# Turning and scaling a normalised tile in one matrix product, in a two-layer-pair transformer kernel

## The chip, the cores and the metric

The kernel runs on one core of a Trainium2 chip. The metric is device time in microseconds (us) of one execution. The kernel before takes 2766.55 us, the median of three runs (2766.45 to 2769.73). Its profile comes from one further execution, which took 2766.35 us.

## The reference, cut to what matters

The reference is two transformer blocks over 256 tokens of width 1024, each with two layers. Every layer has a mixer and a second part (cross attention and a lookup of experts in the first block, a gated feed-forward in the second). In front of each of these parts stands a root-mean-square norm:

```python
def rmsnorm(x, g):
    xf = x.astype(jnp.float32)
    y = xf * lax.rsqrt(jnp.mean(xf * xf, axis=-1, keepdims=True) + EPS)
    return (y * g.astype(jnp.float32)).astype(x.dtype)

hn = rmsnorm(h, mix_norm[l])
h = h + short_conv_pool_mixer(hn, ...)      # starts with hn @ w_in
h = h + memory_cross_attn(rmsnorm(h, xattn_norm[l]), ...)
h = h + peer_ffn(rmsnorm(h, peer_norm[l]), ...)
```

Ten such norms are each followed at once by a product of the normed rows with a weight matrix. The result is float32, and the products are made from float32 data.

## The kernel before, in words

The residual `h` lies in SBUF as two row blocks of 128 tokens by 1024. Each float32 operand of a large product is split into a high part (`hi`, `xh`: the value rounded to the matmul's fp32r format) and a low part (`lo`, `xl`: what is left). One product of float32 numbers is then three fp32r products: high by high, high by low, low by high (`mm3`).

A norm (`norm_T`, `norm_steps`) turns `h` from rows of tokens to columns of tokens. For each row block b, every row is scaled by its factor `r` (the reciprocal root, made by a DVE addition in `rstd`, L220, and a power on GpSimd, L221). The scaled block `xn` (128x1024) is then transposed by TensorE in eight pieces of 128x128 (L266), piece k of both blocks going into columns 0 to 255 of one PSUM bank. There are eight banks: mm0, mm1, tp0, tp1, a0 to a3, one for each piece k. After both blocks, `hilo_ps` empties each bank k twice: ScalarE (ACT) writes the high part `xh` with the gain of the norm (L283), then VectorE (DVE) writes the low part `xl` (L284).

Block 0 of `xn` is scaled by DVE alone (L250, 1024 wide). For block 1 the left half is scaled by DVE (L253) and the right half by ACT (L254). The norm of the first mixer has both factors ready when it begins (`done == 2`). The other nine have only that of block 0 (`finish`, which adds the last products to `h`, makes it), and the factor of block 1 is made inside the norm. In the norm in front of the second block's first mixer a closure in `self.second` makes it, with a second power.

Weights come by DMA on SyncE's queue into a ring `raw` of four buffers, and `_split` makes `hi` (ACT, L114) and `lo` (DVE, L117) from them, in rings of three. `w(name, j)` keeps the splits three blocks ahead of use. In the nine norms, one `_split` stands between the factor of block 1 and its scaling: ACT's L114, then both scalings, then DVE's L117.

After a norm comes, in most stages, `columns`: a result of 128 weight columns by 256 tokens in one PSUM bank, accumulated over eight pieces k, with three products for each k (L152, L153, L154 in `mm3`). Its first call follows the norm directly, so its products wait for `xh` and `xl` of each k. The mixer in front of which the closure stands begins instead with products in the other orientation (weights as the moving operand), through `mm3`.

The order on each engine is the order in which the program is written (a manual schedule); a layer under it adds the semaphore waits that data and buffers ask for. No planner chooses the order.

Of the kernel before, what the change touches and what calls it, by code (L numbers as in the profile page):

```python
# [20 lines left out]
F32 = mybir.dt.float32  # L21
# [4 lines left out]
AF = mybir.ActivationFunctionType  # L26
OP = mybir.AluOpType
# [47 lines left out]
class Program:  # L75
# [23 lines left out]
        self.raw[i] = t  # L99
        self.n_dma += 1  # L100

    def _split(self, between=None):
        if self.order is None or self.n_split == len(self.order):
            if between:
                between()
            return
        i = self.n_split
        w = self.order[i][2]
        while self.n_dma <= i:
            self._load()  # L110
        raw = self.raw.pop(i)
        hi = self.ring.tile([128, w], F32R, name="hi", bufs=self.HL)
        lo = self.ring.tile([128, w], F32R, name="lo", bufs=self.HL)
        self.nc.scalar.activation(hi, raw, AF.Copy)  # L114
        if between:
            between()
        self.nc.vector.tensor_tensor(lo, raw, hi.bitcast(F32), OP.subtract)  # L117
        self.split[i] = (hi, lo)
        self.n_split += 1

# [35 lines left out]
    def columns(self, ps, name, j, xT, k_n=8):  # L156

        hi, lo = self.w(name, j, 128 * k_n)
        for k in range(k_n):
            s = slice(k * 128, (k + 1) * 128)  # L160
            self.mm3(ps, hi[:, s], lo[:, s], xT[0][:, k, :], xT[1][:, k, :], k == 0, k == k_n - 1)

    def rows(self, name, ks, xT, acc, gain=None, fine=False):

# [64 lines left out]
    def norm_T(self, src, gain, xn=None, fill=0):  # L229

        hi, lo = [self.act.tile([128, 8, 256], F32R, name=f"x{i}", bufs=1) for i in "hl"]
        done, self.normed = self.normed, 1
        if xn is not None:
            for _ in self.norm_steps(src, gain, hi, lo, self.ss, xn, self.r, done):
                self.fill(fill)
            return hi, lo
        self.n_norm += 1
        with self.tc.tile_pool(name=f"norm{self.n_norm}", bufs=1) as tmp:
            xn = tmp.tile([128, 2, 1024], F32, name="xn")
            for _ in self.norm_steps(src, gain, hi, lo, self.ss, xn, self.r, done):  # L240
                self.fill(fill)
        return hi, lo

    def norm_steps(self, src, gain, hi, lo, ss, xn, r, done=1):

        nc = self.nc
        pss = [(self.ps_mm() if k < 2 else self.ps_tp() if k < 4 else self.ps_a(k - 4))[:, :256] for k in range(8)]
        for b in range(2):
            if b == 0:
                nc.vector.tensor_scalar(xn[:, b], src[:, b], r[:, 1, b:b + 1], None, op0=OP.mult)  # L250
            else:
                def scale():
                    nc.vector.tensor_scalar(xn[:, b, :512], src[:, b, :512], r[:, 1, b:b + 1], None, op0=OP.mult)  # L253
                    nc.scalar.activation(xn[:, b, 512:], src[:, b, 512:], AF.Copy, scale=r[:, 1, b:b + 1])  # L254

                if done < 2:
                    second, self.second = self.second, None
                    if second:
                        second()
                    else:  # L260
                        self.rstd(r, ss, 1)
                    self._split(scale)
                else:
                    scale()
            for k in range(8):
                nc.tensor.transpose(pss[k][:, b * 128:(b + 1) * 128], xn[:, b, k * 128:(k + 1) * 128], self.ident)  # L266
        first = done == 2 and not self.asked
        for k in range(8):
            if first and k in (0, 4):
                self._split()  # L270
            self.hilo_ps(hi[:, k, :], lo[:, k, :], pss[k], gain[:, k:k + 1])
        yield

    def hilo(self, hi, lo, src):
        self.nc.scalar.activation(hi, src, AF.Copy)  # L275
# [463 lines left out]
    def odd_mixer(self, pool):  # L739
# [44 lines left out]
        for j in range(8):  # L784
            if j == 1:
                ps = turned(ckvT)
                for b in range(2):
                    x = ps[:, b * 128:(b + 1) * 128]
                    nc.scalar.activation(ckv[:, b], x, AF.Copy)
                    self.square_sum(self.const.tile([128, 512], BF, name="scr", bufs=2)[:, :128], ckv[:, b], st[:, b:b + 1], 0)  # L790
                self.power(st[:, 2:4], st[:, 0:2], 128)
            next(columns)
            if j == 2:
                for b in range(2):
                    v.scalar_tensor_tensor(ckv[:, b], ckv[:, b], st[:, 2 + b:3 + b], self.kv_norm, op0=OP.mult, op1=OP.mult)
            if j:
                for _ in range(2):
                    next(select, None)
            yield
# [874 lines left out]
```

## Time and profile before

| what | value |
|---|---|
| median of 3 runs | 2766.55 us (2766.45 to 2769.73) |
| the profiled execution | 2766.35 us, span 2764.3 us |
| PE busy | 2691.8 us, 97% |
| DVE busy | 1993.0 us, 72% |
| ACT busy | 1344.7 us, 49% |
| POOL busy | 66.0 us, 2% |
| mean DMA rate | 168 GB/s |

The span runs from the first to the last instruction of the program; the execution's own time is 2.05 us longer. Busy time of an engine is a sum over its instructions; PE is the matmuls of TensorE, PEld its weight loads, POOL is GpSimd, SP is SyncE. In rows of a timeline, "idle before" and an arrow name what the engine waited for.

### The profile page before, as it was taken

The page shows a single profiled execution, that of the slowest core. Times are in us where ns is not written, and L with a number is a line of the kernel's source. Part 1 is how long each engine was busy: PE and PEld are TensorE (multiplying, and loading weights), DVE is VectorE, ACT ScalarE, POOL GpSimd, SP SyncE. Part 2 cuts the span into 40 slices and gives each one's busy share as a digit, 9 for nine tenths or more (in the row PEclk, how much of TensorE's full clock was granted, in tenths as well). Part 3 has the DMA queues.
Part 4 walks back from the last instruction along what each step waited for, and adds up shares of the span by engine and source line. Part 5 has one row for each costly group of instructions (what it writes and reads, how often), then busy time and mean ns, then how long its engine had stood idle before and what let it go on. Part 6 is the DMA issues. An engine that isn't in the chain of part 4 may idle for free.

```text
span 2764.3 us, 50311 instructions
## 1 busy us (share of the span) xinstructions
PE 2691.8 (97%) x20160; PEld 2453.7 (89%) x20160; DVE 1993.0 (72%) x3741; ACT 1344.7 (49%) x2275; POOL 66.0 (2%) x109
## 2 busy tenths in 40 slices
PE   8999999999999999999999999999999889998998
PEld 7889999998888878978999999888887879987997
DVE  7457788898996556855778889899656765557654
ACT  5455445434444555555544543444455554446543
POOL 2000000000000001010000000000000100000000
PEclk9999999999999999999999999999999999999999
DMA  6645555544555556443555554555555525543454
GB/s 225 214 127 170 184 183 178 165 154 162 165 167 187 191 184 197 137 130 124 174 183 183 178 164 152 165 163 166 188 192 177 180 77 179 187 161 100 160 183 145
DMA packets 127338, 463.32 MB, mean 168 GB/s; under 512 B 14912, under 2 KB 15192, under 8 KB 126336
## 3 DMA queue, kind: packets, MB, share of 16 engines
q1 hardware_dynamic: 122688, 445.31, 49.3%
q0 software_dynamic: 3776, 14.40, 1.7%
q8 instruction: 158, 2.59, 0.4%
q14 instruction: 76, 0.62, 0.1%
q10 hardware_dynamic: 640, 0.40, 0.0%
HBM read 456.64 MB, written 3.34 MB: 166 GB/s over the span
## 4 chain that ended last, share of the span: by engine, by line
PE 90%; DVE 4%; ACT 3%; issue 1%; DMA 1%; POOL 0%; POOLq 0%; ACTq 0%; SPq 0%; DVEq 0%
PE mm L152 16%; PE mm L153 16%; PE mm L154 16%; PE a L152 12%; PE a L154 11%; PE a L153 11%; PE tp L704 3%; DVE lo L117 1%; ACT hi L114 1%; PE a L458 1%; DVE ap L485 1%; PE tp L554 1%; ACT ap L487 1%; PE a L996 0%; PE a L446 0%
## 5 line engine op out<-in xcount | busy, mean ns | idle before, releaser
L117 DVE TENSOR_TENSOR lo<-raw,hi 128x1024 fp32r<-128x1024 f32 (+2 forms) x847 | 1033.4, 1221 | 604.0 <-ACT hi L114 600.9
L114 ACT ACTIVATE hi<-raw 128x1024 fp32r<-128x1024 f32 (+2 forms) x847 | 889.6, 1050 | 522.3 <-PE a L154 495.9
L152 PE MATMUL mm<-xh,hi 128*128 128x256 f32 x3584 | 1026.8, 286 | 3.3 <-DVE xl L284 2.6
L153 PE MATMUL mm<-xl,hi 128*128 128x256 f32 x3584 | 1015.3, 283 | 0.5 <-DVE xl L284 0.5
L154 PE MATMUL mm<-xh,lo 128*128 128x256 f32 x3584 | 1014.3, 283 | 0.9 <-DVE lo L117 0.9
L152 PEld LDWEIGHTS mm<-xh,hi 128*128 128x128 f32 x3584 | 688.0, 192 | 7.1 <-DVE xl L284 4.9
L153 PEld LDWEIGHTS mm<-xl,hi 128*128 128x128 f32 x3584 | 688.1, 192 | 0.9 <-DVE xl L284 0.7
L154 PEld LDWEIGHTS mm<-xh,lo 128*128 128x128 f32 x3584 | 687.7, 192 | 1.3 <-DVE lo L117 1.3
L152 PE MATMUL a<-hi,xh 128*128 128x512 f32 x1072 | 424.7, 396 | 1.6 <-ACT xh L275 1.6
L154 PE MATMUL a<-hi,xl 128*128 128x512 f32 x1072 | 418.2, 390 | 0.0
L153 PE MATMUL a<-lo,xh 128*128 128x512 f32 x1072 | 417.0, 389 | 0.0
L580 ACT ACTIVATE A<-mm 128x256 f32<-128x256 f32 x256 | 104.7, 409 | 437.2 <-PE mm L154 437.2
L154 PEld LDWEIGHTS a<-hi,xl 128*128 128x128 f32 x1072 | 201.2, 188 | 43.6 <-DVE xl L276 0.3
L152 PEld LDWEIGHTS a<-hi,xh 128*128 128x128 f32 x1072 | 201.4, 188 | 41.7 <-ACT xh L275 2.0
L153 PEld LDWEIGHTS a<-lo,xh 128*128 128x128 f32 x1072 | 201.6, 188 | 40.1
L696 DVE TENSOR_TENSOR go<-o,gT 128x512 bf16<-128x512 bf16 x384 | 140.3, 421 | 4.4
L704 PEld LDWEIGHTS <-o 128*128 128x128 bf16 x3072 | 96.7, 98 | 19.5 <-issue 16.7
L704 PE MATMUL tp<-go,o 128*128 128x64 bf16 x3072 | 111.8, 193 | 0.0
L276 DVE TENSOR_TENSOR xl<-A,xh 128x256 fp32r<-128x256 f32 x256 | 106.4, 417 | 2.0 <-ACT xh L275 2.0
L275 ACT ACTIVATE xh<-A 128x256 fp32r<-128x256 f32 x256 | 105.9, 415 | 0.0
L691 DVE TENSOR_TENSOR o<-iota,slot 128x1024 bf16<-128x1024 bf16 x128 | 87.6, 685 | 0.0
L709 DVE TENSOR_TENSOR A<-tp,A 128x512 f32<-128x512 f32 x128 | 87.6, 685 | 0.0
(473 smaller groups left out, 2530.8 us busy)
## 6 DMA issues: line engine op xcount, KB each, us to landing
raw<-pu SPq DMA_DIRECT2D x256, 512.0 KB, 3.7
raw<-pv SPq DMA_DIRECT2D x256, 512.0 KB, 4.3
raw<-fgu SPq DMA_DIRECT2D x88, 512.0 KB, 3.3
raw<-fdown SPq DMA_DIRECT2D x44, 512.0 KB, 3.3
raw<-pwq SPq DMA_DIRECT2D x32, 512.0 KB, 3.7
raw<-ein SPq DMA_DIRECT2D x16, 512.0 KB, 5.4
raw<-eout SPq DMA_DIRECT2D x16, 512.0 KB, 3.5
raw<-xwk SPq DMA_DIRECT2D x16, 512.0 KB, 4.4
```

Source lines behind the costliest of these rows:

```text
L114: self.nc.scalar.activation(hi, raw, AF.Copy)
L117: self.nc.vector.tensor_tensor(lo, raw, hi.bitcast(F32), OP.subtract)
L152: mm(out, ah, bh, start=start, stop=False)
L153: mm(out, ah, bl, start=False, stop=False)
L154: mm(out, al, bh, start=False, stop=stop)
L275: self.nc.scalar.activation(hi, src, AF.Copy)
L276: self.nc.vector.tensor_tensor(lo, src, hi.bitcast(F32), OP.subtract)
L580: self.nc.scalar.activation(A[:, c // 2, :, c % 2], ps, AF.Gelu_apprx_tanh)
L691: v.tensor_tensor(o2, iota[:, None].to_broadcast([128, 8, 64, 2]), slot[:, 1, t, None].to_broadcast([128, 8, 64, 2]), OP.is_equal)
L696: v.tensor_tensor(go[:, k], o1, gT[:, k, t, None].to_broadcast([128, 8, 32, 2]), OP.mult)
L704: nc.tensor.matmul(ps[:, j, :], o2[:, j].rearrange("p n two -> p (n two)"), go[:, k, j].rearrange("p n two -> p (n two)"), start=k == 0, s ...
L709: v.tensor_tensor(a, prod.pop(i).rearrange("p t (c two) -> p t c two", two=2), a, OP.mult)
```

## The change

Instead of scaling a row block and transposing it, the norm multiplies each 128x128 piece of `h`, as it is, with a diagonal matrix of the 128 factors. The product turns and scales the piece in one. DVE makes the diagonal (128x128) from the identity matrix and `r`. The eight pieces now lie in four PSUM banks (tp0, tp1, a0, a1), two to a bank: pieces 0 and 1 in the first, 2 and 3 in the second. The low part of the one weight block that is split inside the norm is made by GpSimd instead of DVE, and ACT no longer scales anything. In `columns`, the product with the low part of x comes one piece later than before, and the product with the low part of the weight takes its place.

```diff
@@ -99,10 +99,8 @@
         self.raw[i] = t
         self.n_dma += 1
 
-    def _split(self, between=None):
+    def _split(self, engine=None):
         if self.order is None or self.n_split == len(self.order):
-            if between:
-                between()
             return
         i = self.n_split
         w = self.order[i][2]
@@ -112,9 +110,7 @@
         hi = self.ring.tile([128, w], F32R, name="hi", bufs=self.HL)
         lo = self.ring.tile([128, w], F32R, name="lo", bufs=self.HL)
         self.nc.scalar.activation(hi, raw, AF.Copy)
-        if between:
-            between()
-        self.nc.vector.tensor_tensor(lo, raw, hi.bitcast(F32), OP.subtract)
+        (engine or self.nc.vector).tensor_tensor(lo, raw, hi.bitcast(F32), OP.subtract)
         self.split[i] = (hi, lo)
         self.n_split += 1
 
@@ -156,9 +152,14 @@
     def columns(self, ps, name, j, xT, k_n=8):
 
         hi, lo = self.w(name, j, 128 * k_n)
+        mm = self.nc.tensor.matmul
         for k in range(k_n):
             s = slice(k * 128, (k + 1) * 128)
-            self.mm3(ps, hi[:, s], lo[:, s], xT[0][:, k, :], xT[1][:, k, :], k == 0, k == k_n - 1)
+            mm(ps, hi[:, s], xT[0][:, k, :], start=k == 0, stop=False)
+            mm(ps, lo[:, s], xT[0][:, k, :], start=False, stop=False)
+            if k:
+                mm(ps, hi[:, (k - 1) * 128:k * 128], xT[1][:, k - 1, :], start=False, stop=False)
+        mm(ps, hi[:, s], xT[1][:, k, :], start=False, stop=True)
 
     def rows(self, name, ks, xT, acc, gain=None, fine=False):
 
@@ -231,45 +232,38 @@
         hi, lo = [self.act.tile([128, 8, 256], F32R, name=f"x{i}", bufs=1) for i in "hl"]
         done, self.normed = self.normed, 1
         if xn is not None:
-            for _ in self.norm_steps(src, gain, hi, lo, self.ss, xn, self.r, done):
-                self.fill(fill)
+            self.norm_steps(src, gain, hi, lo, xn[:, 0, :256].rearrange("p (b t) -> p b t", b=2), self.r, done)
+            self.fill(fill)
             return hi, lo
         self.n_norm += 1
         with self.tc.tile_pool(name=f"norm{self.n_norm}", bufs=1) as tmp:
-            xn = tmp.tile([128, 2, 1024], F32, name="xn")
-            for _ in self.norm_steps(src, gain, hi, lo, self.ss, xn, self.r, done):
-                self.fill(fill)
+            self.norm_steps(src, gain, hi, lo, tmp.tile([128, 2, 128], F32, name="diag"), self.r, done)
+            self.fill(fill)
         return hi, lo
 
-    def norm_steps(self, src, gain, hi, lo, ss, xn, r, done=1):
+    def norm_steps(self, src, gain, hi, lo, diag, r, done):
+
 
         nc = self.nc
-        pss = [(self.ps_mm() if k < 2 else self.ps_tp() if k < 4 else self.ps_a(k - 4))[:, :256] for k in range(8)]
+        banks = [self.ps_tp() if k < 2 else self.ps_a(k - 2) for k in range(4)]
+        pss = [banks[k // 2][:, k % 2 * 256:k % 2 * 256 + 256] for k in range(8)]
         for b in range(2):
-            if b == 0:
-                nc.vector.tensor_scalar(xn[:, b], src[:, b], r[:, 1, b:b + 1], None, op0=OP.mult)
-            else:
-                def scale():
-                    nc.vector.tensor_scalar(xn[:, b, :512], src[:, b, :512], r[:, 1, b:b + 1], None, op0=OP.mult)
-                    nc.scalar.activation(xn[:, b, 512:], src[:, b, 512:], AF.Copy, scale=r[:, 1, b:b + 1])
-
-                if done < 2:
-                    second, self.second = self.second, None
-                    if second:
-                        second()
-                    else:
-                        self.rstd(r, ss, 1)
-                    self._split(scale)
+            if b >= done:
+                second, self.second = self.second, None
+                if second:
+                    second()
                 else:
-                    scale()
+                    self.rstd(r, self.ss, 1)
+                self._split(self.nc.gpsimd)
+            nc.vector.tensor_scalar(diag[:, b], self.ident, r[:, 1, b:b + 1], None, op0=OP.mult)
             for k in range(8):
-                nc.tensor.transpose(pss[k][:, b * 128:(b + 1) * 128], xn[:, b, k * 128:(k + 1) * 128], self.ident)
+                nc.tensor.matmul(pss[k][:, b * 128:(b + 1) * 128], src[:, b, k * 128:(k + 1) * 128], diag[:, b],
+                                 start=True, stop=True)
         first = done == 2 and not self.asked
         for k in range(8):
             if first and k in (0, 4):
                 self._split()
             self.hilo_ps(hi[:, k, :], lo[:, k, :], pss[k], gain[:, k:k + 1])
-        yield
 
     def hilo(self, hi, lo, src):
         self.nc.scalar.activation(hi, src, AF.Copy)
```

On ACT, in the norm in front of the last feed-forward part, one `xh` for each piece. Before (`xn` is the scaled block, the first names of the reads are PSUM banks):

```order
L114 ACTIVATE hi_29069<-raw_28832 128x1024 [waits DMAHW3_49,PE_49]
L254 ACTIVATE xn_29049<-h_71,rstd_29001 128x512 [waits Pool_49]
L283 ACTIVATE xh_29044<-mm1_29050,g_g_ffn_182 128x256 [waits PE_49]
L283 ACTIVATE xh_29044<-mm0_29051,g_g_ffn_182 128x256 [waits PE_49]
L283 ACTIVATE xh_29044<-tp0_29052,g_g_ffn_182 128x256 [waits PE_49]
L283 ACTIVATE xh_29044<-tp1_29053,g_g_ffn_182 128x256 [waits PE_49]
```

The same place on ACT now:

```order
L112 ACTIVATE hi_29020<-raw_28787 128x1024 [waits DMAHW3_49,PE_49]
L277 ACTIVATE xh_28999<-tp0_29005,g_g_ffn_177 128x256 [waits PE_49]
L277 ACTIVATE xh_28999<-tp0_29005,g_g_ffn_177 128x256 [waits DVE_49]
L277 ACTIVATE xh_28999<-tp1_29006,g_g_ffn_177 128x256 [waits PE_49]
L277 ACTIVATE xh_28999<-tp1_29006,g_g_ffn_177 128x256 [waits DVE_49]
L277 ACTIVATE xh_28999<-a0_29007,g_g_ffn_177 128x256 [waits PE_49]
```

The scaling L254 is gone, each bank is now read twice, and the second read of each bank has a wait on DVE where it had one on PE.

On GpSimd, the factors of the last three norms and of the output norm (each `x2` is one power for each row block). Before:

```order
L221 TENSOR_TENSOR rstd_25948<-rstd_25948,mhalf_88 128x1 [waits DVE_49] x2
L221 TENSOR_TENSOR rstd_27895<-rstd_27895,mhalf_88 128x1 [waits DVE_49,Pool_49]
L221 TENSOR_TENSOR rstd_27895<-rstd_27895,mhalf_88 128x1 [waits DVE_49]
L221 TENSOR_TENSOR rstd_29001<-rstd_29001,mhalf_88 128x1 [waits DVE_49] x2
L221 TENSOR_TENSOR rstd_30932<-rstd_30932,mhalf_88 128x1 [waits DVE_49] x2
```

The same place on GpSimd now:

```order
L222 TENSOR_TENSOR rstd_25913<-rstd_25913,mhalf_88 128x1 [waits DVE_49] x2
L113 TENSOR_TENSOR lo_25978<-raw_25750,hi_25977 128x1024 [waits DMAHW7_49,Activation_49,Pool_49]
L222 TENSOR_TENSOR rstd_27855<-rstd_27855,mhalf_88 128x1 [waits DVE_49] x2
L113 TENSOR_TENSOR lo_27921<-raw_27797,hi_27920 128x1024 [waits DMAHW1_49,Activation_49,Pool_49]
L222 TENSOR_TENSOR rstd_28956<-rstd_28956,mhalf_88 128x1 [waits DVE_49] x2
L113 TENSOR_TENSOR lo_29021<-raw_28787,hi_29020 128x1024 [waits DMAHW3_49,Activation_49,Pool_49]
```

The weight's low part now stands on GpSimd right behind the power that makes the factor of block 1, and it waits for ACT's high part.

On PE, the first products of `columns` behind the same norm. Before:

```order
L152 MATMUL mm1_29102<-xh_29044,hi_28993 128x256 [waits DVE_49]
L153 MATMUL mm1_29102<-xl_29045,hi_28993 128x256
L154 MATMUL mm1_29102<-xh_29044,lo_28994 128x256
L152 MATMUL mm1_29102<-xh_29044,hi_28993 128x256 [waits Activation_49]
L153 MATMUL mm1_29102<-xl_29045,hi_28993 128x256 [waits DVE_49]
L154 MATMUL mm1_29102<-xh_29044,lo_28994 128x256
```

The same place on PE now:

```order
L158 MATMUL mm1_29052<-xh_28999,hi_28948 128x256 [waits Activation_49]
L159 MATMUL mm1_29052<-xh_28999,lo_28949 128x256
L158 MATMUL mm1_29052<-xh_28999,hi_28948 128x256 [waits Activation_49]
L159 MATMUL mm1_29052<-xh_28999,lo_28949 128x256
L161 MATMUL mm1_29052<-xl_29000,hi_28948 128x256 [waits DVE_49]
```

The first product now waits for ACT alone, and the product with `xl` of a piece stands behind two products of the next piece.

## Rows read from the trace of the kernel before

**Rows 1.** The page: the span, and the chain of work that ended last, by engine.
```profile
span 2764.3 us, 50311 instructions
...
PE 90%; DVE 4%; ACT 3%; issue 1%; DMA 1%; POOL 0%; POOLq 0%; ACTq 0%; SPq 0%; DVEq 0%
```

**Rows 2.** Timeline, last feed-forward norm: start us, duration us, engine, line, operation, operands.
```profile
2565.03 1.04 ACT L114 ACTIVATE hi<-raw 128x1024 fp32r<-128x1024 f32 x1
...
2565.45 0.55 POOL L221 TENSOR_TENSOR rstd<-rstd,mhalf 128x1 f32<-128x1 f32 x1 [2.04 <-DVE rstd L220]
...
2566.04 0.49 DVE L253 TENSOR_SCALAR xn<-h,rstd 128x512 f32<-128x512 f32 x1 [0.66 <-POOL rstd L221]
2566.44 1.22 DVE L117 TENSOR_TENSOR lo<-raw,hi 128x1024 fp32r<-128x1024 f32 x1
...
2566.58 0.44 PE L266 MATMUL mm<-ident,xn 128*128 128x128 f32 x2 [0.40 <-DVE xn L253]
...
2566.95 0.84 ACT L283 ACTIVATE xh<-mm,g_g_ffn 128x256 fp32r<-128x256 f32 x2 [0.19 <-PE mm L266]
...
2567.57 0.87 DVE L284 SCALAR_TENSOR_TENSOR xl<-mm,g_g_ffn,xh 128x256 fp32r<-128x256 f32 x2
...
2569.14 1.65 DVE L284 SCALAR_TENSOR_TENSOR xl<-a,g_g_ffn,xh 128x256 fp32r<-128x256 f32 x4
...
2571.19 0.29 PE L152 MATMUL mm<-xh,hi 128*128 128x256 f32 x1
```

**Rows 3.** Stages: bounds, length, busy (count) of PE, PEld, DVE, ACT, POOL, PEclk, DMA, GB/s.
```profile
8.68:16.30 7.62, 7.00 (x40) 6.40 (x39) 6.38 (x13) 6.59 (x12) 7.25 (x11) 1.00 0.83 275
138.48:143.77 5.29, 4.91 (x38) 4.28 (x37) 4.85 (x10) 4.04 (x10) 0.00 (x0) 1.00 0.54 185
205.91:211.10 5.19, 4.38 (x35) 3.94 (x33) 4.99 (x11) 4.74 (x11) 0.15 (x1) 1.00 0.75 289
...
1244.53:1250.48 5.95, 5.50 (x35) 5.38 (x33) 5.63 (x11) 4.74 (x11) 0.00 (x0) 0.71 0.28 88
...
2144.56:2147.00 2.44, 1.76 (x10) 1.67 (x9) 2.23 (x5) 1.88 (x5) 2.21 (x5) 0.50 0.06 14
...
2469.41:2475.54 6.13, 5.79 (x36) 5.15 (x35) 6.04 (x12) 4.74 (x11) 0.00 (x1) 0.72 0.28 86
2566.00:2571.19 5.19, 4.36 (x34) 3.94 (x33) 4.99 (x11) 4.98 (x12) 0.00 (x1) 1.00 0.34 104
```

**Rows 4.** Timeline of DVE, window attention: scaling of a 128x128 tile.
```profile
2484.51 0.29 DVE L498 TENSOR_SCALAR ap<-ap,ast 128x128 f32<-128x128 f32 x1
```

**Rows 5.** Timeline of PE, cross attention: plain float32 products of 128 columns.
```profile
170.46 1.28 PE L458 MATMUL a<-apT,V 128*128 128x128 f32 x10
```

**Rows 6.** Timeline, window attention: two halves of one PSUM bank, copied by ACT and DVE.
```profile
2478.90 0.22 ACT L300 ACTIVATE vS<-tp 128x64 f32<-128x64 f32 x1
2479.15 0.22 DVE L301 COPY vS<-tp 128x64 f32<-128x64 f32 x1 [0.82 <-ACT vS L300]
2479.41 0.22 ACT L300 ACTIVATE vS<-tp 128x64 f32<-128x64 f32 x1 [0.29 <-DVE vS L301]
```

**Rows 7.** One line's instructions (L929, GpSimd sums): ns min/median/max, forms.
```profile
L929 POOL TENSOR_TENSOR ba<-bias,add x16: 454/739/1723, 1083.5 to 1194.8; 128x128 f32<-128x128 f32 x8, 128x256 f32<-128x256 f32 x8
```

**Rows 8.** Timelines at three places: a GpSimd operation beside a DVE scaling.
```profile
7.52 0.74 DVE L250 TENSOR_SCALAR xn<-h,rstd 128x1024 f32<-128x1024 f32 x1
7.68 0.99 POOL L221 TENSOR_TENSOR rstd<-rstd,mhalf 128x1 f32<-128x1 f32 x1 [0.90 <-DVE rstd L220]
...
1151.88 0.74 POOL L929 TENSOR_TENSOR ba<-bias,add 128x256 f32<-128x256 f32 x1 [4.75 <-DVE ast L497]
1151.91 0.80 DVE L498 TENSOR_SCALAR ap<-ap,ast 128x128 f32<-128x128 f32 x1
...
1184.05 0.64 DVE L498 TENSOR_SCALAR ap<-ap,ast 128x256 f32<-128x256 f32 x1
1184.09 0.45 POOL L929 TENSOR_TENSOR ba<-bias,add 128x128 f32<-128x128 f32 x1 [1.43 <-DVE ast L497]
```

## The prediction

> **What bounds the kernel now.** I read the page first, then the timeline of one norm, then the stages between a norm's last factor and the second column of products behind it, and at the end single lines for the prices. The chain that ended last is PE for 90% [rows 1]: a product saved or delayed on PE is saved or delayed in the end. PE waits in few places, and the ten norms are among them, because everything behind a norm needs its result. The reader should see in [rows 2] the chain of a plain norm. GpSimd's power ends at 2566.00 (2565.45 and 0.55). DVE scales at 2566.04, the first transpose of block 1 starts at 2566.58, ACT's first `xh` at 2566.95, DVE's first `xl` at 2567.57, and the second column of products starts at 2571.19. That is 5.19 us from the power, the length of that stage in [rows 3]. There are five such plain stages of 5.18 to 5.19 us, of which the first and the last are shown. In between, PE follows the evictions: DVE's last four `xl` end at 2570.79 (2569.14 and 1.65), 0.40 before the second column.
>
> The other five are the very first norm (8.68), the first cross attention (138.48), two in which the granted clock fell, with a mean of 0.71 and 0.72 (1244.53 and 2469.41), and the one whose factor takes a second power (2144.56, at 0.50, the lower of the two levels, 1.2 GHz) [rows 3].
>
> **The change part by part.** *The scaling.* L253, L254 and L250 go; two diagonals of 128x128 come. A DVE scaling of that shape took 0.29 us [rows 4] against 0.49 for L253 [rows 2]. The diagonal of block 1 starts 0.04 behind the power as L253 did, so it ends at 2566.33, and the first product starts 0.05 later, at 2566.38: 0.20 us won. The diagonal of block 0 lies beside the sums of block 1 and decides nothing.
>
> *The products.* Sixteen plain float32 products replace sixteen transposes. Ten of them with 128 columns took 1.28 us [rows 5]; with 0.27 for the last one alone that is a step of 0.11, so eight take about 0.9 us and cost what transposes cost. The Trainium skill, page "TensorE: Matmul & The Clock Gate", section Terms, speaks against this: it calls the transpose mode four times faster for FP32. By that rule a product would take some 0.43 us as an estimate (four steps of 0.11), and the second product of each bank would come about 0.3 us later in each norm, some 3 us in all ten. The row disagrees, and the sum goes by the row.
>
> *The banks.* This is the term that decides. Two pieces now share a bank, and in the order on ACT the second `xh` of each bank waits for DVE. In the trace two halves of one bank were copied in the same manner: ACT at 2478.90, DVE at 2479.15, ACT again at 2479.41, each 0.03 or 0.04 after the end of the other (0.22 each) [rows 6]. So the reads of a bank go in turns, ACT, DVE, ACT, DVE, while before, with a bank for each piece, ACT ran ahead. One `xl` takes 0.48 and each further one 0.39 (two in 0.87, four in 1.65); an `xh` by the same division of 0.84 takes 0.46 [rows 2]. A pair is then `xl` 0.48, a gap of 0.03, `xh` 0.46, a gap of 0.03, and 0.40 until the next bank's first `xl` can follow: 1.40 us for two pieces, against 0.78 before.
>
> The plain norm comes out so. First product 2566.38; the bank must be written fully, so 0.11 for the second product and 0.37 from a product's start to `xh` (2566.58 to 2566.95): `xh` at 2566.86. First `xl` at 2567.35 (0.46 and 0.03). Three pairs of 1.40 bring 2571.55. The last pair, up to the end of its second `xl` (0.48, 0.03, 0.46, 0.03, 0.48), brings 2573.03. The second column follows 0.28 later, not 0.40, since one product instead of two stands behind the last `xl`: 2573.31, or 7.31 us from the power. Against 5.19 that is 2.12 us lost.
>
> *The low part one piece later.* It lets the first products start on `xh` alone, and saves the 0.12 just counted. In all later columns nothing waits, the products are as many, and each loads its weights as before (34 products, 33 loads [rows 3]); cost nothing. If the new order slowed each product, no cover would exist, as PE is the bound.
>
> *The weight's low part on GpSimd.* DVE loses L117 (1.22 us, 2566.44 to 2567.66), which held back the first `xl`; that gain is in the 2567.35. On GpSimd 128 columns took 0.454 and 256 took 0.74 [rows 7, 8], 2.23 ns a column, so 1024 take about 2.45 us. It starts when ACT's L114 is done (2566.07) and ends near 2568.6; the second column, which reads it first, starts at 2573.31. So it is hidden unless it disturbs DVE. Behind it on GpSimd wait only loads and later factors. Bounds for a disturbed `xl`: no row shows a DVE operation that reads PSUM beside a long GpSimd one; at least nothing, at most a wait to 2568.6 for the first `xl`, 1.25 us in each norm. I take nothing, because the bank's gaps already stand in that time.
>
> *The exceptional norms.* The first cross attention: 7.31 less 5.29 is 2.0. The very first norm has the same pairs: 2.1. In the two with a fallen clock, six products at 1.2 GHz take 1.28 us (six times 256 columns), less than a pair; so 7.31 less 5.95 and less 6.13, 1.4 and 1.2. In the one with two powers, ACT's high part is long ready, so GpSimd begins the low part (832 columns, 2.0 us by the same slope) straight behind the power, ahead of DVE, which still has one small operation to do before the diagonal. [Rows 8] shows what then happens: L498 started 0.03 behind GpSimd's L929 and took 0.80 instead of 0.29, ending 0.09 after it. The diagonal comes about 1.6 late; its products in the other orientation use pieces more slowly than the pairs deliver; 0.4 come back from the missing L254. I take 1.2, between nothing and 2.0.
>
> Sum: five times 2.12 is 10.6; with 2.0, 2.1, 1.4, 1.2 and 1.2 it is 18.5. The profiled execution took 2766.35, 0.2 below the median of 2766.55: 2784.85, so 2785.
>
> **The rivals.** *A: GpSimd takes DVE's port in the other norms too.* In the plain norm L114 ends at 2566.07, 0.03 after the diagonal starts at 2566.04 [rows 2]: a race. A lead of 0.16 for DVE was enough once (7.52 against 7.68: the power had to wait and took 0.99 instead of 0.55), a lead of 0.04 was not (1184.05 against 1184.09: the scaling took 0.64, the GpSimd sum ran undisturbed) [rows 8]. The lead here is 0.03 plus whatever GpSimd needs to start behind ACT, so between the two. If it is lost, the diagonal ends 0.09 after GpSimd, at 2566.07 and 2.45 and 0.09, 2568.61 instead of 2566.33: 2.3 us in each norm. Three lost give 2792, seven 2801. The Trainium skill says the same on the page "SBUF — State Buffer", section "SBUF: two separate sides": whichever of the two starts first holds the shared port pair for its whole instruction. The rows agree.
>
> *B: the clock.* With the pairs, PE stands half idle for over five us in each norm, more than before, and a norm with a fallen clock was 0.76 and 0.94 longer than a plain one [rows 3]. If seven more norms leave the pairs at the lower level and pay 0.9 after it, that is 6.3 us: 2791. Against it: five of ten held the clock through a longer full stop.
>
> *C: not slower.* The wait on DVE in the order finds its operation done, or the bank does not take turns. Then the `xl` run on at 0.39: from 2567.35 seven steps and 0.48 bring 2570.56 and the second column at 2570.84, 0.35 earlier than before. Nine norms win 3.2, the one with two powers loses 1.2: 2764. It is decided by one point: whether the second `xh` of a bank starts 0.38 or 0.97 behind the first. Against it stand [rows 6].
>
> **How the numbers follow.** The forecast has 0.58, with its own range 2780 to 2790 (a pair of 1.30 to 1.50, the norm with two powers at either bound). A has 0.25, B 0.10, C 0.07. The range 2779 to 2801 holds the forecast, B and most of A, and leaves out C and the upper end of A. About 0.2%, 5.5 us, is what can be told from no change: C lies within it. Slower 0.92, same 0.06, faster 0.02.
>
> **What would show it.** Right: in each norm ACT's `xh` come in steps of about 0.97 and 0.4 in turn, `xl` idle before every second one with ACT as the releaser, and 7.3 us from power to second column. GpSimd's low part takes about 2.45. Diagonals of 0.29; in the norm with two powers one near 2 us, and such long ones in other norms would show A. B would show as a granted clock below 1 behind norms that had 1.00. Wrong at the root: `xh` in even steps of 0.38, or a step between later products of a column that differs from before, which moves the time by far more than the norms.

## The result and the profile after

The changed kernel takes 2797.53 us (median of four runs, 2796.3 to 2798.44) against 2767.39 for the kernel before (four runs): a ratio of 1.0104, with a 95% interval of 1.0092 to 1.0117. It is 30.1 us slower. The forecast was 2785, with 2780 to 2790 as its own range, so its sign and its mechanism held and its size was too small. The time lies within the stated 2779 to 2801 only because that range reached towards another case, which did not occur. The profiled execution took 2798.44 us, 32.1 more than the one of before.

The page of the changed kernel, span, engines and chain, beside [rows 1]:

```profile
span 2796.7 us, 50628 instructions
...
PE 2720.1 (97%) x20320; PEld 2477.9 (89%) x20320; DVE 1982.8 (71%) x3732; ACT 1344.0 (48%) x2265; POOL 86.2 (3%) x118
...
PE 89%; DVE 5%; ACT 3%; issue 1%; DMA 1%; POOL 0%; POOLq 0%; SPq 0%; ACTq 0%; DVEq 0%
```

The line of the engines on the page of before:

```profile
PE 2691.8 (97%) x20160; PEld 2453.7 (89%) x20160; DVE 1993.0 (72%) x3741; ACT 1344.7 (49%) x2275; POOL 66.0 (2%) x109
```

The chain is PE's as before. PE has 20320 matmul records; the page of before has 20160. That is 160 more, and 160 transposes (ten norms, two blocks, eight pieces) became 160 plain products: each plain float32 product is two records, called two passes below, and each transpose was one.

The timeline of the last feed-forward norm (columns as in [rows 2], to which it answers):

```profile
2595.29 0.56 POOL L222 TENSOR_TENSOR rstd<-rstd,mhalf 128x1 f32<-128x1 f32 x1 [2.04 <-DVE rstd L221]
...
2595.88 0.29 DVE L258 TENSOR_SCALAR diag<-ident,rstd 128x128 f32<-128x128 f32 x1 [0.67 <-POOL rstd L222]
2596.04 2.36 POOL L113 TENSOR_TENSOR lo<-raw,hi 128x1024 fp32r<-128x1024 f32 x1 [0.20 <-POOL rstd L222]
...
2596.35 1.06 PE L260 MATMUL tp<-diag,h 128*128 128x128 f32 x8
2597.00 0.47 ACT L277 ACTIVATE xh<-tp,g_g_ffn 128x256 fp32r<-128x256 f32 x1 [1.08 <-PE tp L260]
...
2597.50 0.48 DVE L278 SCALAR_TENSOR_TENSOR xl<-tp,g_g_ffn,xh 128x256 fp32r<-128x256 f32 x1 [1.33 <-ACT xh L277]
2598.02 0.84 ACT L277 ACTIVATE xh<-tp,g_g_ffn 128x256 fp32r<-128x256 f32 x2 [0.55 <-DVE xl L278]
...
2598.53 0.88 DVE L278 SCALAR_TENSOR_TENSOR xl<-tp,g_g_ffn,xh 128x256 fp32r<-128x256 f32 x2 [0.54 <-ACT xh L277]
...
2599.44 0.47 ACT L277 ACTIVATE xh<-tp,g_g_ffn 128x256 fp32r<-128x256 f32 x1 [0.58 <-DVE xl L278]
...
2602.78 0.48 DVE L278 SCALAR_TENSOR_TENSOR xl<-a,g_g_ffn,xh 128x256 fp32r<-128x256 f32 x1 [0.54 <-ACT xh L277]
...
2603.55 0.28 PE L158 MATMUL mm<-xh,hi 128*128 128x256 f32 x1
```

The releasers in brackets tell it: ACT's second `xh` of a bank waits for DVE's `xl` (0.55, 0.58), DVE's next `xl` waits for that `xh` (0.54). From one pair to the next are 1.42 us (2598.02 to 2599.44). Before, DVE's eight `xl` followed each other without a wait [rows 2].

The stages from a norm's last power to the second column (columns as in [rows 3]; first norm, first cross attention, first plain norm, second cross attention, two powers, window, last plain norm):

```profile
8.09:20.79 12.70, 10.14 (x56) 9.33 (x56) 6.36 (x12) 6.01 (x11) 11.18 (x18) 0.97 0.75 231
143.76:152.15 8.39, 7.08 (x53) 6.15 (x52) 3.89 (x9) 4.44 (x10) 2.35 (x1) 1.00 0.39 127
214.29:222.01 7.72, 6.41 (x47) 5.48 (x46) 3.88 (x9) 4.31 (x10) 2.51 (x2) 1.00 0.52 195
...
1262.74:1270.41 7.67, 6.35 (x46) 5.43 (x45) 3.88 (x9) 4.32 (x10) 2.39 (x1) 1.00 0.23 71
...
2166.64:2176.80 10.16, 9.29 (x50) 8.62 (x49) 5.79 (x11) 4.31 (x10) 4.57 (x7) 0.81 0.36 107
...
2497.55:2505.33 7.78, 6.47 (x48) 5.54 (x46) 4.11 (x10) 4.33 (x10) 2.35 (x1) 1.00 0.17 67
2595.85:2603.55 7.70, 6.39 (x47) 5.47 (x46) 3.88 (x9) 4.33 (x10) 2.36 (x1) 1.00 0.23 70
```

A plain norm takes 7.7 us, where the prediction had 7.31 and before had 5.19.

The rest lies outside the norms. After the fourth norm the trace of the changed kernel has three stretches at the lower clock that the trace of before has not. First the changed kernel from the start of the third column behind that norm to the last product ahead of the next norm, and the three stretches; then the same part of the kernel before:

```profile
1055.95:1259.91 203.96, 197.90 (x1286) 174.66 (x1285) 136.67 (x261) 107.33 (x202) 19.07 (x25) 0.97 0.45 151
...
1078.16:1081.57 3.41, 3.41 (x19) 3.19 (x17) 2.13 (x4) 0.17 (x2) 0.00 (x0) 0.50 0.48 160
1108.88:1112.29 3.41, 3.41 (x9) 2.27 (x7) 0.45 (x1) 0.00 (x0) 0.00 (x0) 0.50 0.48 155
1129.36:1132.77 3.41, 3.41 (x18) 3.41 (x18) 3.38 (x6) 0.00 (x0) 0.00 (x0) 0.50 0.48 154
```

```profile
1042.51:1241.70 199.19, 193.36 (x1286) 170.70 (x1285) 136.53 (x261) 107.13 (x202) 19.36 (x25) 1.00 0.47 155
```

The same 1286 matmul records take 203.96 us instead of 199.19: 4.8 us in a part where the change alters only the order of a column's products (experiments 3 and 7 price that).

### The profile page after: what moved, and what is told of

It reads as the page before. It is cut to its first block, busy times and chain, and to the rows that moved or that the text cites. A ratio compares the mean times of both kernels' runs of the same rounds, so it can differ in the third digit from the quotient of the medians.

```text
span 2796.7 us, 50628 instructions
## 1 busy us (share of the span) xinstructions
PE 2720.1 (97%) x20320; PEld 2477.9 (89%) x20320; DVE 1982.8 (71%) x3732; ACT 1344.0 (48%) x2265; POOL 86.2 (3%) x118
## 4 chain that ended last, share of the span: by engine, by line
PE 89%; DVE 5%; ACT 3%; issue 1%; DMA 1%; POOL 0%; POOLq 0%; SPq 0%; ACTq 0%; DVEq 0%
PE mm L158 15%; PE mm L159 15%; PE mm L161 13%; PE a L148 12%; PE a L150 11%; PE a L149 11%; PE tp L698 3%; PE mm L162 2%; DVE lo L113 1%; DVE xl L278 1%; ACT hi L112 1%; ACT xh L277 1%; PE tp L260 1%; PE mm L148 1%; PE mm L150 1%
## 5 line engine op out<-in xcount | busy, mean ns | idle before, releaser
L113 DVE TENSOR_TENSOR lo<-raw,hi 128x1024 fp32r<-128x1024 f32 x838 | 1022.8, 1222 | 600.9 <-ACT hi L112 598.0
L158 PE MATMUL mm<-xh,hi 128*128 128x256 f32 x3584 | 1012.3, 288 | 13.7 <-ACT xh L277 12.9
L159 PE MATMUL mm<-xh,lo 128*128 128x256 f32 x3584 | 996.6, 283 | 0.8 <-DVE lo L113 0.8
L161 PEld LDWEIGHTS mm<-xl,hi 128*128 128x128 f32 x3136 | 602.9, 192 | 0.0
L222 POOL TENSOR_TENSOR rstd<-rstd,mhalf 128x1 f32<-128x1 f32 x24 | 13.7, 572 | 2543.1 <-DVE rstd L221 2496.2
```

What stands on the lines that cost most here:

```text
L113: (engine or self.nc.vector).tensor_tensor(lo, raw, hi.bitcast(F32), OP.subtract)
L158: mm(ps, hi[:, s], xT[0][:, k, :], start=k == 0, stop=False)
L159: mm(ps, lo[:, s], xT[0][:, k, :], start=False, stop=False)
L161: mm(ps, hi[:, (k - 1) * 128:k * 128], xT[1][:, k - 1, :], start=False, stop=False)
```

## The experiments

Theory: the reads of a bank by two engines go in turns because the second `xh` waits for the first `xl`. Rivals: GpSimd slows VectorE; the new order of a column slows the products; plain products or half-filled banks cost as such. The table sums up what follows. "Stage" is the last plain norm, from the end of the power to the second column.

| kernel | stage, us | time, us | ratio to before (95%) |
|---|---|---|---|
| before | 5.19 | 2767 to 2768 | |
| changed | 7.70 | 2797.5 | 1.0104 (1.0092 to 1.0117) |
| 1: changed, eight banks | 5.16 | 2773.2 | 1.0017 (1.0008 to 1.0027) |
| 2: changed, low part by DVE, ahead | 8.88 | 2802.6 | 1.0129 (1.0112 to 1.0146) |
| 3: changed, old order | 7.82 | 2797.0 | 1.0108 (1.0091 to 1.0125) |
| 4: changed, neighbours apart | 5.32 | 2772.4 | 1.0017 (1.0008 to 1.0027) |
| 5: before, four banks | 7.72 | 2794.2 | 1.0095 (1.0077 to 1.0113) |
| 6: before, diagonal products | 5.17 | 2771.9 | 1.0015 (1.0005 to 1.0025) |
| 7: before, new order | 5.08 | 2766.7 | 0.9996 (0.9986 to 1.0006) |
| 8: changed, low part by DVE, behind | 7.70 | 2792.8 | 1.0088 (1.0070 to 1.0106) |
| 9: before, 13 us later | 5.18 | 2783.7 | 1.0059 (1.0043 to 1.0074) |
| 10: before, order and GpSimd's low part | 4.97 | 2766.1 | 0.9991 (0.9982 to 1.0000) |

**1. Eight banks.**

```diff
-        banks = [self.ps_tp() if k < 2 else self.ps_a(k - 2) for k in range(4)]
-        pss = [banks[k // 2][:, k % 2 * 256:k % 2 * 256 + 256] for k in range(8)]
+        pss = [(self.ps_mm() if k < 2 else self.ps_tp() if k < 4 else self.ps_a(k - 4))[:, :256] for k in range(8)]
```

> The changed kernel, but each piece of a norm has a bank of its own again (mm0, mm1, tp0, tp1, a0 to a3); diagonal products, GpSimd's low part and the new order of a column stay. Theory (two readers of one bank take turns): the low parts run on at 0.39 us, the second column of a plain norm comes about 4.9 us after the power instead of 7.70 (first low part 1.43 after the power, seven steps of 0.39, 0.48 and 0.29). That is 2.8 us in each of eight norms, with some 1.5 in the first one: about 2774 us, plus or minus 5 for stretches at the lower clock that come and go. Rival 1 (GpSimd's low part slows VectorE): the stage stays above 7.4 us and the time near 2796. Rival 2 (the new order of the column slows the products): the same, near 2797.

Measured 2773.21, as expected, though the parts differ: 2.5 us in a plain norm instead of 2.8, and 3.1 in the first norm (20.79 to 17.70 for its second column) instead of 1.5. The timeline of its last plain norm:

```profile
2570.79 0.88 DVE L277 SCALAR_TENSOR_TENSOR xl<-mm,g_g_ffn,xh 128x256 fp32r<-128x256 f32 x2 [1.11 <-ACT xh L276]
...
2571.56 0.37 PE L158 MATMUL mm<-xh,hi 128*128 128x256 f32 x1
...
2572.36 1.65 DVE L277 SCALAR_TENSOR_TENSOR xl<-a,g_g_ffn,xh 128x256 fp32r<-128x256 f32 x4
...
2574.51 0.28 PE L158 MATMUL mm<-xh,hi 128*128 128x256 f32 x1
```

The `xl` run on without a wait, so GpSimd's low part and the new order are not what cost. But the stage is 5.16 and not the expected 4.93: the last `xl` ends at 2574.01, yet PE, which began the 24 products of the first column at 2571.56, behind its sixteen passes, needs until 2574.51 for them (24 by 0.12 is 2.88). The second pass of each product has eaten what diagonal, order and low part win. Of the 5 us that this kernel is still behind the one before, the traces show 1.4 in the first norm and 0.6 in the first cross attention.

**2 and 8. The weight's low part by DVE**, ahead of the diagonal and behind it.

```diff
# 2
-                self._split(self.nc.gpsimd)
+                self._split()
# 8, in the place of 2
-                self._split(self.nc.gpsimd)
             nc.vector.tensor_scalar(diag[:, b], self.ident, r[:, 1, b:b + 1], None, op0=OP.mult)
+            if b >= done:
+                self._split()
```

> The changed kernel, but the weight's low part inside a norm is made by VectorE again, behind the diagonal of block 1; two pieces to a bank, diagonal products and new order stay. Theory (turns at the bank): the low part fits in before the first xl (ends about 1.59 us after the power, xl starts at 1.65), so a plain norm stays at 7.7 us; the norm with two powers loses its stuck VectorE operation and gets about 1.7 us shorter: about 2796 us. Rival 1 (GpSimd slows VectorE): plain norms fall to 5.2 to 6 us, the time to about 2780.

Measured 2802.60: missed. The expectation had the order wrong, as the last plain norm shows:

```profile
2599.10 1.23 DVE L113 TENSOR_TENSOR lo<-raw,hi 128x1024 fp32r<-128x1024 f32 x1 [0.73 <-ACT hi L112]
2600.24 0.28 DVE L258 TENSOR_SCALAR diag<-ident,rstd 128x128 f32<-128x128 f32 x1
...
2601.33 0.47 ACT L277 ACTIVATE xh<-tp,g_g_ffn 128x256 fp32r<-128x256 f32 x1 [2.26 <-PE tp L260]
```

The low part stands ahead of the diagonal, so the factor, ready at 2599.00, waits until 2600.24. The eighth experiment moves it behind:

> The changed kernel, the weight's low part by VectorE as in the second experiment, but written behind the diagonal of block 1 and not ahead of it. Theory (what cost 1.17 us in each norm there was the low part's place ahead of the diagonal; behind it VectorE has 1.33 us to spare, the low part takes 1.23): plain norms as in the changed kernel, 7.7 us; the norm with two powers loses the stuck operation, 1.7 us: 2795 us, plus or minus 4 for the clock. Rival (VectorE's low part costs as such, GpSimd's relief is worth a microsecond in each norm): plain norms 8.9 us as in that experiment, 2803.

```profile
2589.97 0.29 DVE L257 TENSOR_SCALAR diag<-ident,rstd 128x128 f32<-128x128 f32 x1 [0.66 <-POOL rstd L222]
2590.17 1.22 DVE L113 TENSOR_TENSOR lo<-raw,hi 128x1024 fp32r<-128x1024 f32 x1
...
2591.59 0.48 DVE L279 SCALAR_TENSOR_TENSOR xl<-tp,g_g_ffn,xh 128x256 fp32r<-128x256 f32 x1 [0.21 <-ACT xh L278]
```

The stage is 7.70 again: the cost was the place, and with pairs GpSimd's relief is worth nothing. In the norm with two powers the small operation that was stuck takes 0.16 again, but PE there was still busy with block 0 at the lower clock, and the first `xh` comes only 0.64 earlier instead of the 1.7 expected. The time, 2792.79, cannot be told from the 2792.10 of the changed kernel's second trace, which has fewer stretches at the lower clock than its first (11 below).

**3 and 7. The order of a column.** In 3 `columns` has the three lines of `mm3` again, in 7 the kernel before has the new ones.

> The changed kernel, but each column's products in the order of before (high by high, high by low, low by high for each piece). Theory (turns at the bank): in a norm two products instead of one stand behind the last xl, 0.12 us each time: a plain norm 7.8 us, about 2798.5 us in all; steps between products of later columns stay 0.120. Rival 2 (the new order slows products): steps differ, and the time falls by 10 us or more.

> The kernel before with one part of the change: the new order of a column's products. Theory: one product less behind the last xl, 0.12 us in each norm that a column follows, some 1 us in all, 2767 us; steps between later products stay 0.120. Rival (the order slows products): 2775 or more.

Measured 2797.02 and 2766.66; stages 7.82 (0.12 more) and 5.08 (0.11 less). The step between the products of later columns stays 0.120 in all. Rival 2 falls, and the order is worth about 1 us, which the time cannot tell from nothing.

**4. Neighbours in different banks**, still four.

```diff
-        pss = [banks[k // 2][:, k % 2 * 256:k % 2 * 256 + 256] for k in range(8)]
+        pss = [banks[k % 4][:, k // 4 * 256:k // 4 * 256 + 256] for k in range(8)]
...
-            for k in range(8):
+            for k in (0, 4, 1, 5, 2, 6, 3, 7):
                 nc.tensor.matmul(pss[k][:, b * 128:(b + 1) * 128], ...
```

> The changed kernel, still four banks, but a bank holds pieces k and k+4 instead of two neighbours, and the products are made in the order 0, 4, 1, 5, 2, 6, 3, 7, so that a bank is full as early as now. Theory (only neighbours in one bank take turns): the second reading of a bank by ScalarE finds VectorE's first long done; the low parts run on at 0.39 us, and the second column of a plain norm comes about 5.2 us after the power (1.65, seven steps of 0.39, 0.48, 0.29): about 2.5 us less in each of eight norms, 2777 us plus or minus 5 for the clock. Rival 3 (four banks cost as such, since a bank is written and read in two halves): near 7.7 us and 2797.

```profile
2573.25 0.92 ACT L277 ACTIVATE xh<-tp,g_g_ffn 128x256 fp32r<-128x256 f32 x2 [1.08 <-PE tp L260]
...
2573.76 0.93 DVE L278 SCALAR_TENSOR_TENSOR xl<-tp,g_g_ffn,xh 128x256 fp32r<-128x256 f32 x2 [1.33 <-ACT xh L277]
...
2574.96 0.83 ACT L277 ACTIVATE xh<-tp,g_g_ffn 128x256 fp32r<-128x256 f32 x2
```

Measured 2772.35, stage 5.32. The third and fourth pair of `xh`, in banks that DVE has been through once, start without a wait. So two neighbours in one bank are what costs. Four banks as such cost little here, 0.16 against the 5.16 of experiment 1, but 1.4 in the first norm (its second column at 19.05 instead of 17.70).

**5. Four banks alone**, in the kernel before (the edit of 1 the other way).

> The kernel before with one part of the change: four banks with two neighbouring pieces each; scaled rows, transposes, VectorE's low part and the old order of a column stay. Theory (turns at the bank): the first xl stays at 1.57 us after the power, held by the weight's low part; then three pairs of 1.42, 1.01, 0.48 and 0.40 bring the second column to 7.72 instead of 5.19: 2.5 us in each of eight norms, about 2 in the first, 2790 us, plus or minus 4 for the clock. Rival (the turns come from the plain products writing a bank, not from reading it twice): 5.3 us and 2769.

```profile
2591.34 0.47 ACT L284 ACTIVATE xh<-tp,g_g_ffn 128x256 fp32r<-128x256 f32 x1 [0.30 <-PE tp L267]
2591.86 0.48 DVE L285 SCALAR_TENSOR_TENSOR xl<-tp,g_g_ffn,xh 128x256 fp32r<-128x256 f32 x1
...
2592.37 0.84 ACT L284 ACTIVATE xh<-tp,g_g_ffn 128x256 fp32r<-128x256 f32 x2 [0.56 <-DVE xl L285]
```

Measured 2794.23, just beyond the expected range, and a stage of 7.72, the expected figure: this one part, with transposes and the old order, reproduces nearly the whole loss.

**6. Diagonal products alone** (the code of 8, with eight banks and the old order).

> The kernel before with one part of the change: the diagonal products in place of scaling and transposing; eight banks, old order, VectorE makes the weight's low part, behind the diagonal of block 1. Theory (a plain float32 product is two passes of 0.11 us, a transpose one): a plain norm stays at about 5.2 to 5.3 us, since eight passes more fit beside the evictions but leave no gain from the shorter diagonal; the first norm, in which a pass takes 0.21, loses 1.8 to 2.4: 2771 us, plus or minus 4 for the clock. The prediction's term (products cost what transposes cost): the first norm loses nothing, 2767.

Measured 2771.92, stage 5.17. The third column of the first norm starts at 19.76 instead of 19.18, 0.6 late and not 1.8 to 2.4: a miss, since with eight banks most of the slow passes fit beside the evictions. That the time came out near the expected 2771 all the same is luck: of the 4 us the norms show 0.6 here and 0.6 in the first cross attention, and this trace has eight stretches at 0.50 where the two traces of the kernel before have six and five.

**9, 11 and 12. The clock.** Experiment 9 adds eighteen scalings to the first norm of the kernel before (`for _ in range(18 if done == 2 else 0)` around L250); 11 and 12 are the changed kernel and the one before once more.

> The kernel before, untouched in its norms, with the scaling of block 0 in the first norm done 18 times more (0.74 us each), so that everything behind stands about 13.3 us later, which is as late as the odd mixer stands in the changed kernel. Theory (stretches at the lower clock fall on other places when the program shifts, whatever the norms do): in the mixer behind the fourth norm one to three stretches of 3.41 us at 0.50, where the trace of before had none; the time 2781 us plus up to 5. Rival (they come from what the changed norms do): none there, 2781 us.

> The changed kernel once more, for its stretches at the lower clock. Theory (they differ from one execution to the next): the norms as before, 7.7 us for a plain one, but other places or another number of stretches than 1078, 1108 and 1129 us in the fourth norm's mixer. Rival (they belong to the kernel): the same three within 1 us.

> The kernel before once more, for the same question. Theory (the stretches differ from one execution to the next): the stages of the plain norms 5.19 us again, but one or more stretches at 0.50 in the fourth norm's mixer or none in one of the two norms that had one (1245 and 2470 us). Rival (they belong to the kernel): the same four stretches.

The changed kernel took 2792.10 this time, and between its fourth and fifth norm no stretch is at the lower clock (the part that took 203.96 above):

```profile
1054.93:1253.67 198.74, 193.08 (x1287) 170.61 (x1284) 136.66 (x261) 107.31 (x202) 19.27 (x25) 1.00 0.47 155
```

Its plain norms are 7.7 as before. The kernel before, at 2765.66, now had one stretch in that part (at 1112) and none in the two norms that had one, whose stages became 5.19. Experiment 9 had one (at 1127). So these stretches come and go between executions of one kernel, and some 5 us of the first comparison are theirs. What decides where they fall was not found. The four runs of the first comparison lie within 2.2 us of each other and all over 4 us above this repeat, so the session or the chip may have a part in it; that was not tested.

One stretch comes with the pairs, the one behind the first norm. Here it is in the changed kernel's two traces:

```profile
20.02:23.43 3.41, 3.41 (x17) 3.41 (x18) 2.90 (x7) 2.08 (x3) 0.00 (x0) 0.50 0.98 328
18.05:21.46 3.41, 3.41 (x16) 3.27 (x17) 2.43 (x6) 2.47 (x5) 1.84 (x4) 0.50 0.78 254
```

It stands in all six traces of kernels with neighbours in one bank (the changed one twice, 2, 3, 5 and 8; it starts between 18.0 and 20.7) and in none of the eight others.

**10. What is left as a gain.**

```diff
-                    self._split(scale)
+                    self._split(scale, None if second else nc.gpsimd)
```

with the new `columns`, on the kernel before.

> What the experiments leave as a gain: the kernel before with eight banks, scaled rows and transposes, and of the change only the new order of a column and GpSimd's low part inside a norm (VectorE's in the norm with two powers). Theory: the first xl starts 0.13 us earlier (1.44 after the power instead of 1.57) and one product less stands behind the last xl (0.12): a plain norm 4.94 us instead of 5.19, some 2 us in all, 2766 against 2768, less than can be told from no change by the time alone; the stage in the trace tells it. Rival (GpSimd's low part takes VectorE's port while block 1 is scaled): the scaling takes over 0.6 us, and a plain norm gets longer than 5.19.

```profile
2566.20 0.49 DVE L258 TENSOR_SCALAR xn<-h,rstd 128x512 f32<-128x512 f32 x1 [0.67 <-POOL rstd L226]
2566.36 2.55 POOL L117 TENSOR_TENSOR lo<-raw,hi 128x1024 fp32r<-128x1024 f32 x1 [0.20 <-POOL rstd L226]
...
2567.62 0.88 DVE L289 SCALAR_TENSOR_TENSOR xl<-mm,g_g_ffn,xh 128x256 fp32r<-128x256 f32 x2 [0.93 <-ACT xh L288]
```

The scaling keeps its 0.49, the stage is 4.97, and eleven runs have a median of 2766.09: 0.9991, with an interval that ends at 1.0000. With 7 it is one of two versions below the kernel before in time and stage. Its 2 us are at the edge of what the time can tell from nothing.

## Why the prediction was too low

Between the two first traces the spans differ by 32.4 us (2796.7 less 2764.3). Taken from the last product ahead of each norm to the second column, and for the norm with two powers to the 49th product behind its transposes, the norms account for 25.7 of them:

| term | predicted | measured |
|---|---|---|
| five plain norms | 10.6 | 12.7 |
| first cross attention | 2.0 | 2.6 |
| first norm | 2.1 | 4.5 |
| second cross attention | 1.4 | 1.7 |
| window | 1.2 | 1.7 |
| two powers | 1.2 | 2.5 |
| the rest, outside the norms | 0 | 6.7 |

- **The banks: right.** A pair takes 1.42 (1.40 predicted), and experiments 1, 4 and 5 show it as the cause from both sides. So rival C did not occur: the second `xh` of a bank starts 1.02 behind the first (2597.00, 2598.02), where 0.97 was to decide against C.
- **The products: wrong, and the first step that failed.** "Sixteen plain float32 products ... cost what transposes cost" took the ten records of [rows 5] for ten products. They are five: the code of that line asks for 64 products in the two cross attentions, and the trace has 128 records. Each product is two passes of 0.11. So block 0 keeps PE busy until 2596.35, and the first product of block 1 starts 0.50 behind the power instead of 0.38; then four passes and not two fill the first bank. The first `xh` comes 1.15 after the power (2595.85 to 2597.00) instead of 0.86. With 1.42 for 1.40 three times and some 0.03 at the end that makes 7.70 of 7.31. The Trainium skill, page "TensorE: Matmul & The Clock Gate", section Terms, sets the transpose mode four times faster for FP32. The row was read as speaking against it; the records show a factor of two, so the direction was the page's and its size was not.
- **The first norm: mis-sized.** There a pass takes 0.23 (eight in 1.86, 7.70 to 9.56), and twenty of them stand ahead of the first `xh`, which comes at 12.37, against 10.54 before. The pairs that follow have a low part of 1.23 between them on DVE. With eight banks the change loses 1.4 there (experiment 1), with four banks and neighbours apart 2.7 (4), with neighbours together 4.5; the four banks alone lose 3.4 (5). So the passes, the number of banks and the neighbours all have a part. A stretch at the lower clock (from 20.02) adds 1.1 behind the second column; with the 4.8 shown above that is most of the rest.
- **The norm with two powers: right on the stuck operation, wrong on the rest.** GpSimd's low part starts ahead of DVE, and a 128x1 operation takes 1.89 instead of 0.16:

```profile
2166.61 1.95 POOL L113 TENSOR_TENSOR lo<-raw,hi 128x832 fp32r<-128x832 f32 x1
2166.68 1.89 DVE L1081 TENSOR_TENSOR rstd<-rstd 128x1 f32<-128x1 f32 x1 [0.66 <-POOL rstd L216]
...
2168.60 0.28 DVE L258 TENSOR_SCALAR diag<-ident,rstd 128x128 f32<-128x128 f32 x1
```

  It was the small operation ahead of the diagonal that was stuck, not the diagonal, for 1.73 (1.89 less 0.16) where about 1.6 were foreseen. The norm lost 2.5 (1.9 in the repeated traces); the prediction took 1.2, with 2.0 as upper bound. Two terms stood at nothing there: the pairs, which taken alone cost 0.8 (experiment 5: 20.53 us for this norm against 19.71, with about 7 us at 0.50 in both), and the second passes, part of them at the lower clock, which no run prices there alone.
- **Rival A: did not occur** in the other eight norms that have GpSimd's low part. In the last one GpSimd started 0.16 behind DVE's diagonal (2596.04, 2595.88), a lead that sufficed in [rows 8] too; over the eight the lead was 0.09 to 1.02, and every diagonal of block 1 kept its 0.29. That "the rows agree" with the rule of the first to start was too much: in one of the three of [rows 8] DVE started 0.04 ahead and was held all the same (0.64).
- **Rival B: true of one norm in ten.** The plain norms all kept 1.00. Behind the first norm a stretch fell that was not there before, and it comes with the pairs (six traces of six, above); it is worth the 1.1. The three in the mixer behind the fourth norm belong to the execution. The two norms with a fallen clock, priced at 1.4 and 1.2, were an accident of the one trace: in two traces without it they differ by 2.5 and 2.6 (10.50 less 8.00; 10.59 less 7.99).
- **The low part on GpSimd: right.** It takes 2.36 us (2.45 estimated), each `xl` beside it takes 0.48 as elsewhere, and nothing is won (experiment 8). The order of a column was right too: 0.12 in a norm, nothing in later columns (3 and 7).

In the repeated traces (11 less 12) the spans differ by 26.6 (2790.3 less 2763.7), nearly all of it in the norms.

## What to carry to other kernels

When two engines empty a PSUM tile in turn and the program makes each reader of a bank wait for the one before it, neighbours in the pipeline belong in different banks: which pieces share a bank decided more here (2.4 us of a plain norm) than how many banks there are (0.16). Before a duration is divided by a count, check whether the count is of instructions or of passes: compare it with the loops of the code. And a clock that falls in a stage in a single trace is no term of a sum before a second trace shows it too.

## What was not expected of the hardware

- A plain float32 product of 128 columns shows as two records of 0.11 us; a float32 transpose of the same size shows as one.
- DVE's `xl`, which reads PSUM, kept 0.48 us beside a GpSimd operation of 2.36, while a 128x1 operation from SBUF to SBUF waited for one to its end (1.89 for 0.16).
- Two executions of one kernel differ by 6.4 us in span (2796.7, 2790.3), 5.2 of it in one part with three stretches of 3.41 us at a granted clock of 0.50 in the one and none in the other.
- No run here shows what two engines would do that read one bank at the same time: the wait between them is the program's, and no kernel here ran without it.
